# One encoder layer on one core: scaling the second group's rows in another stage, squares in a tile of their own, refills at other steps

## The chip, the core and the metric

The kernel runs on one core of a Trainium2 chip. The core has a matmul engine (TensorE, PE in the profile), VectorE (DVE), ScalarE (ACT), GpSimd (POOL) and SyncE (SP), which here issues nearly all DMA transfers. The engines run side by side. Each works through its own list of instructions in order, and an instruction that waits for a semaphore holds back all that stand behind it on that engine. SBUF is the memory on the chip, PSUM the accumulators that matmuls write, DRAM the memory outside.

The metric is the device time of one execution in microseconds (us), as the median of several runs. Before the change three runs took 1821.98, 1823.78 and 1827.82 us.

## The reference

One layer of a bidirectional encoder is applied to 1024 tokens (sample) and 256 tokens (prompt), model width 2048, all in float32:

```python
hn = rms_norm(x, norm_g)
proj = hn @ w_in                       # 2048 -> 4896 columns
xbc, z_ssd, dt_raw, q, k, v, z_att, mq, z_mem = split_cols(proj, IN_SIZES)
xbc = silu(centred_dwconv(xbc, conv_w, conv_b))       # 5 taps along the tokens
...                                    # SSD scans both ways, windowed attention,
...                                    # attention over 256 memory rows, gates
return x + concatenate([o_ssd, o_att, o_mem], -1) @ w_out
```

What matters here is the first line. `rms_norm(x, g)` divides each token's row by the root of its mean square plus 1e-6 and multiplies each feature by g. So the sum of squares of each token must be known before the token's features can be scaled for the product with `w_in`. The memory rows have such a norm too.

## The kernel before

**Products in two pieces.** Every operand of a large product is split into a high part (the value rounded to the matmul's reduced float32 form) and a low part (the remainder). A product is three matmuls: high x high, high x low, low x high. For the weights this is `wsplit` (lines 201 to 205): ACT writes the high part `wh`, DVE subtracts and writes the low part `wl`.

**Groups.** The 1280 tokens are worked in two groups of 640. `x_turned` holds x with features first, so a row tile is 128 features x 640 tokens, and there are 16 row tiles per group. `cur["H", q]` and `cur["L", q]`, q = 0 to 3, hold the two parts of four row tiles each.

**Token blocks.** `block_tok` (line 231) makes a product with 512 (or 288) weight columns for 4 or 5 token tiles: for each of 16 steps k it loads a weight tile `wraw` (three buffers), splits it (four buffers `wh` and `wl`), and issues three matmuls for each token tile. The last two steps are taken together.

**Stages of seven products.** `block_pair` (line 1182) makes two 128-column outputs over 640 tokens with a Strassen-like scheme: seven products instead of eight over halves of the features, tokens and columns. It has eight steps k per unit; each step is 21 matmuls of 320 columns. POOL makes three sums of weight tiles for it (`weight_sums`, line 1177, sums in `ws`), and ACT and DVE split them as `sh` and `sl` (three buffers). The sums of the rows, in the same scheme, are made by `p_sums` (line 1270) and split into `tH`, `tL` by `p_split` (lines 1276 and 1277). One stage has ten units (`units`, four gates and six convolution outputs), and there is one stage for each group. The evacuation of a unit (`ev_seven`) puts its first product into a tile `yu` of the pool `fin`, tag `xst`, with one buffer. The taps and gates of a unit are put into a list `left` and are issued a few at a time beside the next units.

**Order of the stages that the change touches.** Two memory blocks (`w_mem`); the q block of the first group, during which the rows of the first group are scaled and split (`p_step`); the first stage of seven products; the kv block and the mq block of the first group (token blocks), during which the rows of the second group are scaled, stored, summed and split (`t_step`), and in the end the first stage's rows in `cur` are replaced by those of the second group; the second stage of seven products. Then follow attention, SSD and the output products, which the change leaves alone.

**What feeds the second group's rows.** `stage_stats` reads the tokens of the second group (five tiles) and the memory rows (four tiles) in 36 pieces of 128 x 512, and ACT squares each with a running sum (line 1392). The piece lies in the same one buffer as `yu`. It is advanced at five of the seven points of each unit. When it is through, `x_rows(1)` spreads the reciprocal roots over a tile `rbc` (128 x 640). In the kv and mq blocks `p_load` then loads two row tiles of x, `p_scale` multiplies them by the gain and by `rbc` on DVE (line 1237) and stores them in DRAM (`xs_d`), `p_sums` and `p_split` follow. Later `r_load` reads the scaled rows back from `xs_d` and `r_fill` splits them into `cur` (lines 1248 and 1249), into new tiles. `t_plan` says at which step each of these is called.

**What sets the order.** The program is written step by step, but a scheduler of the tile framework sets the final order on each engine from the program's order, raised priorities (`tc.high_priority`) and its own idea of what is ready; `tc.issue_after(marks)` keeps an instruction behind the last weight split. A tile with one buffer makes the next writer wait for all readers of the last content.

Of the kernel before, what the change touches and what calls it, by code (L numbers as in the profile page):

```python
# [19 lines left out]
P = 128  # L20
# [21 lines left out]
def hymba_encoder_kernel(  # L42
# [223 lines left out]
    def block_feat(name, evac):  # L266

        ps = [[acc.tile([P, 512], F32, tag="acc", name="acc") for _ in range(2)] for _ in range(2)]
        src = laid_in(name)
        hls = {}  # L270
        for kk in range(KT // 2):
            raw = wp.tile([P, 512], F32, tag="wraw", name="wraw", bufs=RB)
            S.dma_start(raw, src[kk])
            with tc.high_priority(offset=HP[2]):
                h = wp.tile([P, 2, 256], F32R, tag="wh", name="wh", bufs=WB)
                l = wp.tile([P, 2, 256], F32R, tag="wl", name="wl", bufs=WB)
                wsplit(raw, h.rearrange("p a c -> p (a c)"), l.rearrange("p a c -> p (a c)"))
            hls[kk] = h, l
            if kk == KT // 2 - 2:
                continue  # L280
            tail = kk == KT // 2 - 1

            for kks in ([(kk - 1, kk)] if tail else [(kk,)]):
                for f in range(2):
                    for k in [2 * x + j for x in kks for j in range(2)]:
                        q, m = divmod(k, 4)
                        sh, sl = [x[:, k % 2, f * P:(f + 1) * P] for x in hls[k // 2]]
                        for half in range(2):
                            c = slice(half * 320, half * 320 + 320)
                            o = ps[f][half][:, :320]  # L290
                            T.matmul(o, sh, cur["H", q][:, m, c], start=(k == 0), stop=False)
                            T.matmul(o, sh, cur["L", q][:, m, c], start=False, stop=False)
                            T.matmul(o, sl, cur["H", q][:, m, c], start=False, stop=(k == KT - 1))
                    if tail and f == 0:
                        with tc.high_priority(offset=HP[1]):
                            evac(0, ps[0])
            for k in range(2 * kks[0], 2 * kk + 2):
                yield k
        with tc.high_priority(offset=HP[1]):
            evac(1, ps[1])  # L300


    def ev_gate(c, base):
# [5 lines left out]
        return f  # L309

    def ev_gateT(c, grp, f0):
        def f(fc, ps):
            z = ev.tile([P, 640], F32, tag="evu", name="zs")
            for b in range(2):
                zb, p = z[:, b * 320:b * 320 + 320], ps[b][:, :320]
                A.activation(zb, p, AF.Tanh, scale=0.5)
                V.scalar_tensor_tensor(out=zb, in0=zb, scalar=1.0, in1=p, op0=ALU.add, op1=ALU.mult)
            S.dma_start(zT_d[c][grp][:, f0 + fc, :], z)
        return f
# [24 lines left out]
    def conv_work(grp, fc, u):  # L344
# [5 lines left out]
        def first_tap():  # L350
            c.append(ev.tile([P, 650], F32, tag="evt", name="c")[:, :n])
            A.activation(c[0], u[:, :n], AF.Identity, scale=cw[0], bias=vec[:, R_CB + fc:R_CB + fc + 1])
# [26 lines left out]

    def ev_conv(grp, f0):  # L380
        us = []

        def f(fc, ps):
            fc = f0 + fc
            u = ev.tile([P, 650], F32, tag="evu", name="u")
            V.tensor_copy(u[:, 0:4], carry[:, fc, :])
# [6 lines left out]
            if len(us) == 2:  # L393
                left.extend(conv_two(*[conv_work(grp, f0 + i, us[i]) for i in range(2)]))
# [1369 lines left out]
```

## Time and profile before

| what | value |
|---|---|
| median of 3 runs | 1823.78 us (1821.98 to 1827.82) |
| the profiled execution | 1824.83 us |
| its span, first to last instruction | 1823.1 us |
| PE busy | 1778.3 us, 98% |
| DVE, ACT, POOL busy | 73%, 52%, 37% |
| granted PE clock, mean | 0.995 |
| DMA moved | 328.96 MB, 180 GB/s |

The profile is one execution. The page gives the busy time of each engine, a picture in 40 slices, the DMA queues, the chain of work that ended last, and the costliest groups of instructions. A group reads: line, engine, operation, output <- inputs, shape, number | busy us, mean ns of one | idle time of the engine just before them, and what ended it. A wait reads: who <- what ended it: us in total, times, longest. A row of the table of stretches reads: stretch in us, its length, then for each engine the busy us and the number of instructions, then the granted PE clock, the DMA share and GB/s. Matmuls are pipelined, so "busy" is not yet peak; the number of matmuls in a stretch shows better how fast they go.

### The profile page before, as it was taken

The numbers are of one execution on the slowest core, as the hardware profiler recorded it, in microseconds if no ns is written. First come the engines' busy times: TensorE is split into PE (matmuls) and PEld (weight loads), VectorE is DVE, ScalarE is ACT, GpSimd is POOL, SyncE is SP. The second block draws the span as 40 slices with busy tenths as digits, with TensorE's granted clock in tenths as the row PEclk, the third lists the DMA queues.
The fourth block names the chain that finished last, engine by engine and source line by source line (L and its number), as shares of the span: only waits on it lengthen the run. The fifth ranks groups of instructions, "written<-read, shape, count | busy, mean of one in ns | idle before, by whom it ended". The sixth has DMA issues, their size and how long they took to land.

```text
span 1823.1 us, 30989 instructions
## 1 busy us (share of the span) xinstructions
PE 1778.3 (98%) x10306; PEld 1572.7 (86%) x10306; DVE 1328.4 (73%) x2473; ACT 950.1 (52%) x2081; POOL 673.6 (37%) x1092
## 2 busy tenths in 40 slices
PE   9999999999999999999999999999999999999999
PEld 7788999999799999987777877887777787889998
DVE  5595678888878889787667767767787765766665
ACT  6554545553454444366567447666547644543332
POOL 0115778870168889411001110001111101048774
PEclk9999999999999999999999999999999999999999
DMA  8685544446853343374545577656688765654442
GB/s 296 196 315 192 152 142 146 128 146 206 265 189 91 114 117 110 106 219 133 162 136 155 165 241 267 207 173 213 220 282 259 238 212 161 201 154 147 142 139 81
DMA packets 213873, 328.96 MB, mean 180 GB/s; under 512 B 21904, under 2 KB 84688, under 8 KB 213712
## 3 DMA queue, kind: packets, MB, share of 16 engines
q1 hardware_dynamic: 213568, 326.92, 57.8%
q8 instruction: 81, 1.33, 0.3%
q14 instruction: 80, 0.66, 0.1%
q10 hardware_dynamic: 144, 0.06, 0.0%
HBM read 250.29 MB, written 76.61 MB: 179 GB/s over the span
## 4 chain that ended last, share of the span: by engine, by line
PE 65%; DMA 12%; issue 8%; DVE 6%; POOL 5%; ACT 3%; SPq 1%; ACTq 0%; POOLq 0%; DVEq 0%
PE acc L257 8%; PE acc L256 8%; PE acc L258 8%; PE acc L1207 7%; PE acc L1205 7%; PE acc L1206 7%; POOL ws L1177 3%; PE accm L1206 3%; PE accm L1205 3%; PE accm L1207 3%; PE py L937 2%; DVE wl L204 1%; DMA wraw<-in_w_in_pairs_dram 1%; DMA rf<-ac 1%; POOL wraw L1177 1%
## 5 line engine op out<-in xcount | busy, mean ns | idle before, releaser
L257 PE MATMUL acc<-wl,xH 128*128 128x512 f32 (+1 forms) x1248 | 479.0, 384 | 8.0 <-DVE wl L204 7.7
L256 PE MATMUL acc<-wh,xH 128*128 128x512 f32 (+1 forms) x1248 | 484.3, 388 | 1.6 <-ACT wh L203 1.5
L258 PE MATMUL acc<-wh,xL 128*128 128x512 f32 (+1 forms) x1248 | 476.0, 382 | 0.0
L204 DVE TENSOR_TENSOR wl<-wraw,wh 128x512 fp32r<-128x512 f32 (+1 forms) x480 | 351.8, 736 | 145.7 <-ACT wh L203 140.5
L203 ACT ACTIVATE wh<-wraw 128x512 fp32r<-128x512 f32 (+1 forms) x480 | 290.8, 612 | 211.1 <-PE acc L258 126.7
L257 PEld LDWEIGHTS acc<-wl,xH 128*128 128x128 f32 x1248 | 236.1, 189 | 54.9 <-DVE wl L204 13.6
L256 PEld LDWEIGHTS acc<-wh,xH 128*128 128x128 f32 x1248 | 236.1, 189 | 45.7 <-ACT wh L203 3.6
L258 PEld LDWEIGHTS acc<-wh,xL 128*128 128x128 f32 x1248 | 235.7, 189 | 42.1 <-issue 0.7
L1177 POOL TENSOR_TENSOR ws<-wraw 128x128 f32<-128x128 f32 x224 | 144.8, 646 | 340.9 <-DMA wraw<-in_w_in_pairs_dram 210.2
L203 ACT ACTIVATE sh<-ws 128x384 fp32r<-128x384 f32 x224 | 115.7, 523 | 272.9 <-PE acc L1206 131.2
L204 DVE TENSOR_TENSOR sl<-ws,sh 128x384 fp32r<-128x384 f32 x224 | 156.2, 700 | 136.9 <-ACT sh L203 132.5
L1177 POOL TENSOR_TENSOR ws<-wraw,ws 128x128 f32<-128x128 f32 x224 | 149.1, 666 | 17.3
L1177 POOL TENSOR_TENSOR ws<-ws,wraw 128x128 f32<-128x128 f32 x224 | 152.8, 682 | 0.0
L1177 POOL TENSOR_TENSOR wraw<-wraw 128x128 f32<-128x128 f32 x224 | 138.9, 620 | 17.5
L645 POOL COPY lg<-nsink 128x2 f32<-128x2 f32 x40 | 17.3, 433 | 268.9 <-PE ppt L673 138.9
L1205 PE MATMUL acc<-xH,wh 128*128 128x320 f32 x320 | 99.5, 311 | 3.7 <-ACT wh L203 3.7
L1207 PE MATMUL acc<-xH,wl 128*128 128x320 f32 x320 | 99.2, 310 | 3.3 <-DVE wl L204 3.3
L1205 PE MATMUL acc<-tH,sh 128*128 128x320 f32 x320 | 99.1, 310 | 1.0 <-ACT qs L324 1.0
L1207 PE MATMUL acc<-tH,sl 128*128 128x320 f32 x320 | 99.2, 310 | 0.0
L1206 PE MATMUL accm<-tL,wh 128*128 128x320 f32 x320 | 99.1, 310 | 0.0
L1205 PE MATMUL accm<-tH,wh 128*128 128x320 f32 x320 | 99.0, 310 | 0.0
L1206 PE MATMUL acc<-xL,wh 128*128 128x320 f32 x320 | 99.0, 309 | 0.0
(479 smaller groups left out, 3921.1 us busy)
## 6 DMA issues: line engine op xcount, KB each, us to landing
wraw<-in_w_in_pairs_dram SPq DMA_DIRECT2D x160, 256.0 KB, 2.8
wraw<-in_w_in_laid_dram SPq DMA_DIRECT2D x128, 256.0 KB, 3.7
wraw<-in_w_out_laid_dram SPq DMA_DIRECT2D x64, 256.0 KB, 3.3
wraw<-in_w_out_pairs_dram SPq DMA_DIRECT2D x64, 256.0 KB, 2.9
xH<-xH SPq DMA_DIRECT2D x16, 640.0 KB, 5.9
xL<-xL SPq DMA_DIRECT2D x16, 640.0 KB, 6.5
rf<-ac SPq DMA_DIRECT2D x40, 256.0 KB, 4.0
rb<-ac SPq DMA_DIRECT2D x40, 256.0 KB, 4.4
```

The costliest lines, as they stand in the source:

```text
L203: a = A.activation(h, raw, AF.Copy)
L204: b = V.tensor_sub(l, raw, h.bitcast(F32))
L256: T.matmul(ps[t][:, :n], sh, h[:, :n], start=(k_ == 0), stop=False)
L257: T.matmul(ps[t][:, :n], sh, l[:, :n], start=False, stop=False)
L258: T.matmul(ps[t][:, :n], sl, h[:, :n], start=False, stop=(k_ == last))
L645: G.tensor_copy(lg[:, :, nk:nk + 1], ns8[:, rr, :].unsqueeze(2))
L937: T.matmul(py[:, h * 64:h * 64 + 64], mt[:, (h % 4) * P:(h % 4 + 1) * P], xsT[g][:, h * 64:h * 64 + 64], start=True, stop=True)
L1177: G.tensor_tensor(out=o, in0=x, in1=y, op=op)
L1205: T.matmul(ps[p], h, xh, start=(k_ == 0), stop=False)
L1206: T.matmul(ps[p], h, xl, start=False, stop=False)
L1207: T.matmul(ps[p], l, xh, start=False, stop=(k_ == 7))
```

## The change

- The squares get a tile of their own (tag `sq`, one buffer) and are made in two lots: the five token tiles of x beside the first stage of seven products (`first_side`), the four memory tiles beside the second (`next_side`). They are advanced one piece at a time with no grouping. In the first stage the side work is advanced at five points of a unit in the first four units and at seven in the other six; in the second stage at three.
- After its squares, `first_side` runs `x_rows(1)` and then, for each of the 16 row tiles, loads it from `x_turned` into the tile `sq`, scales it on DVE, and stores it in `xs_d`.
- In the kv and mq blocks the second group's rows are loaded from `xs_d` instead of `x_turned` (`p_next`), and neither scaled nor stored there. In the plan the loads of the first four pairs stay where they are and those of the other four come one step earlier; the sums of the first four stay, the others come one step earlier; the splits of the first four come one step later, the others stay; the refills stand at steps 25, 26, 27, 28, 29, 31, 33 and 35 instead of 25, 27, 29, 31, 32, 33, 35 and 37, and they write into the tiles that are there.
- Within one step the calls are sorted: split, refill, sums, loads.
- Three functions that nothing calls are taken out (`block_feat`, `ev_gateT`, `ev_conv`); small tiles move from the pool `sm` to `mp`, and some tiles of 650 columns become 646 or 640.

```diff
-    def p_load(k, grp=0):
+    def p_load(k, src):
         raw[k] = [rp.tile([P, 640], F32, tag="ch", name=n, bufs=CH) for n in ("ra", "rb_")]
         for i in range(2):
-            r = k + 8 * i
-            S.dma_start(raw[k][i], x_turned[grp, r * P:(r + 1) * P, :])
-
-    def p_scale(k, grp=0):
-
-        for i, x in enumerate(raw[k]):
-            r = k + 8 * i
-            V.scalar_tensor_tensor(out=x, in0=x, scalar=vec[:, R_G + r:R_G + r + 1], in1=rbc, op0=ALU.mult, op1=ALU.mult)
-            if grp:
-                S.dma_start(xs_d[r], x)
-
-    def p_rows(k, tiles):
+            S.dma_start(raw[k][i], src(k + 8 * i))
+
+    def x_row(grp, r):
+        return x_turned[grp, r * P:(r + 1) * P, :]
+
+    def scale_row(r, x):
+        V.scalar_tensor_tensor(out=x, in0=x, scalar=vec[:, R_G + r:R_G + r + 1], in1=rbc, op0=ALU.mult, op1=ALU.mult)
+
+    def p_rows(k, tiles, new=True):
         for i, x in enumerate(tiles):
             q, j = divmod(k + 8 * i, 4)
-            if j == 0:
+            if new and j == 0:
                 new_quad(q)
...
     def r_fill(k):
-        p_rows(k, again.pop(k))
+        p_rows(k, again.pop(k), new=False)
...
+    def p_first(k):
+        p_load(k, lambda r: x_row(0, r))
+
+    def p_next(k):
+        p_load(k, lambda r: xs_d[r])
...
     t_plan = {}
     for k in range(8):
-        at = (3, 6, 9, 12, 15, 17, 19, 21)[k]
-        for j, f in ((at - 2, lambda k: p_load(k, 1)), (at, lambda k: p_scale(k, 1)), (at + 1, p_sums), (at + 2, p_split)):
+        at = (4, 7, 10, 13, 15, 17, 19, 21)[k]
+        for j, f in ((at - 3, p_next), (at, p_sums), (at + 2, p_split)):
             t_plan.setdefault(j, []).append((f, k))
-    for k, at in enumerate((25, 27, 29, 31, 32, 33, 35, 37)):
+    for k, at in enumerate((25, 26, 27, 28, 29, 31, 33, 35)):
         for j, f in ((at - 2, r_load), (at, r_fill)):
             t_plan.setdefault(j, []).append((f, k))
...
-    def stage_stats():
-        yield from stats([(xrow(t), t) for t in range(5, 10)] + [(mrow(i), 10 + i) for i in range(4)],
-                         lambda i: fin.tile([P, 512], F32, tag="xst", name="sst"), ahead=1, group=3)
+    def square_place(_):
+        return fin.tile([P, 640], F32, tag="sq", name="sst")[:, :512]
+
+    def first_side():
+        yield from stats([(xrow(t), t) for t in range(5, 10)], square_place, ahead=1)
+        for _ in x_rows(1):
+            yield
+        for r in range(KT):
+            x = fin.tile([P, 640], F32, tag="sq", name="xrow")
+            S.dma_start(x, x_row(1, r))
+            yield
+            with ExitStack() as st:
+                for ins in marks:
+                    st.enter_context(tc.issue_after(ins))
+                scale_row(r, x)
+                S.dma_start(xs_d[r], x)
+            yield
+
+    def next_side():
+        yield from stats([(mrow(i), 10 + i) for i in range(4)], square_place, ahead=1)
...
-    def pairs_in(grp, extra):
+    def pairs_in(grp, extra, side):
...
-                if k in (0, 2, 4, 5, 7):
-                    next(squares, None)
+                if grp == 0 and (u > 3 or k not in (3, 7)) or grp and k in (0, 2, 4):
+                    next(side, None)
...
-    pairs_in(0, p_step)
-    for _ in squares:
-        pass
-    for _ in x_rows(1):
-        pass
+    side = first_side()
+    pairs_in(0, p_step, side)
```

More of the change, by code (lines that the diff above doesn't have):

```diff
@@ L264, in block_tok @@
             yield k
[L266 to L300, printed above, removed]
     def ev_gate(c, base):
@@ L308, in f @@
             S.dma_start(z_d[c][base + i], z)
[L309 to L318, printed above, removed]
         return f
@@ L1251, in p_fill @@
     def p_fill(k):
-        p_scale(k)
+        for i, x in enumerate(raw[k]):
+            scale_row(k + 8 * i, x)
         p_rows(k, raw[k])
@@ L1312, in t_step @@
                 weight_sums(w_in_pairs, (j - 27) // 2)
-            for f, k in t_plan.get(j, ())[::-1]:
+            for f, k in sorted(t_plan.get(j, ()), key=lambda x: ((p_split, r_fill, p_sums, p_next, r_load).index(x[0]), x[1])):
                 f(k)
@@ L1330, in begin @@
             else:
-                tiles = [ev.tile([P, 650], F32, tag="evu", name="r") for _ in range(2)]
+                tiles = [ev.tile([P, 640], F32, tag="evu", name="r") for _ in range(2)]
             r0, r1 = [hv(x[:, o:o + 640], 2) for x in tiles]
@@ L1579, in hymba_encoder_kernel @@
         extra=left_and(lambda k: t_step(16 + k)))
-    pairs_in(1, t_step)
+    side = next_side()
+    pairs_in(1, t_step, side)
+    assert next(side, None) is None
     early.close()
```

47 lines of the change are left out of this document (16 added, 31 removed).

## The prediction

> **What bounds the kernel now.** I read the engine totals first, then a table of stretches cut at the stages, then who waited for whom in the stretches that the change touches, and last single instructions there.
>
> ```profile
> span 1823.1 us, 30989 instructions
> PE 1778.3 (98%) x10306; PEld 1572.7 (86%) x10306; DVE 1328.4 (73%) x2473; ACT 950.1 (52%) x2081; POOL 673.6 (37%) x1092
> ```
>
> TensorE (PE) is the bound; whatever is gained must come out of the 45 us in which it does not work. The next table (stretch in us from the start of the span; busy us and number of instructions of each engine; granted clock; DMA share; GB/s) holds, in order, the second memory block, the q block, the first unit of the first stage of seven products, its units two to four, its units five to ten, the kv block, the mq block, and the second stage of seven products.
>
> ```profile
> 60.00:93.00 33.00, 32.53 (x146) 25.92 (x145) 22.19 (x38) 19.17 (x38) 2.77 (x6) 1.00 0.68 211
> 93.00:147.00 54.00, 53.18 (x234) 43.42 (x232) 46.77 (x77) 27.20 (x44) 9.34 (x12) 1.00 0.87 307
> 147.00:172.00 25.00, 22.70 (x138) 21.11 (x138) 10.85 (x19) 12.58 (x25) 13.64 (x23) 1.00 0.64 211
> 172.00:250.00 78.00, 76.90 (x521) 75.96 (x520) 53.72 (x86) 38.48 (x79) 58.35 (x98) 1.00 0.50 145
> 250.00:405.00 155.00, 149.03 (x995) 146.68 (x994) 126.32 (x190) 80.72 (x165) 130.46 (x201) 0.99 0.47 137
> 405.00:442.00 37.00, 37.00 (x278) 37.00 (x277) 28.63 (x51) 13.16 (x26) 3.96 (x7) 1.00 0.53 162
> 442.00:510.00 68.00, 62.19 (x265) 49.05 (x264) 55.15 (x85) 29.93 (x50) 13.43 (x20) 0.95 0.84 276
> 510.00:757.00 247.00, 247.00 (x1687) 246.63 (x1686) 206.01 (x330) 115.93 (x205) 199.78 (x296) 1.00 0.39 115
> ```
>
> The second stage of seven products loses nothing: 1687 matmuls in 247 us, 0.1464 us each, so 21 of them, one step k of a unit, are 3.07 us. At that pace the 521 matmuls of units two to four need 76.3 of their 78 us (lost: 1.7) and the 995 of units five to ten 145.7 of 155 (lost: 9.3). The mq block idles 5.8 us and runs at a granted clock of 0.95, another 3.4 us of 68: 9.2. The other stretches idle 0.5, 0.8, 2.3 and 0. Together 23.8 us lie in reach of this change, 1.3%.
>
> What PE waits for there is the weight split on ScalarE (ACT, line 203) and VectorE (DVE, line 204):
>
> ```profile
> PE acc L257 <- DVE wl L204: 6.5, 10, 1.4
> PE acc L1205 <- ACT wh L203: 3.7, 5, 1.2
> PE acc L1207 <- DVE wl L204: 3.3, 7, 0.8
> ```
>
> In the first stage the split is late behind the squares of stage_stats. The first row is their group between 145 and 440 us; then three squares with their waits, and the matmul that stood after them:
>
> ```profile
> L1392 ACT ACTIVATE sst<-sst 128x512 f32<-128x512 f32 x36 | 22.7, 631 | 53.7 <-DMA sst<-in_mem_sample_dram 14.8 <-DMA sst<-in_x_sample_dram 13.8 <-DMA sst<-in_mem_prompt_dram 12.3
> ...
> 190.91 0.63 ACT L1392 ACTIVATE sst<-sst 128x512 f32<-128x512 f32 x1 [3.65 <-DMA sst<-in_x_sample_dram]
> ...
> 194.72 0.63 ACT L1392 ACTIVATE sst<-sst 128x512 f32<-128x512 f32 x1 [2.15 <-DMA sst<-in_x_sample_dram]
> ...
> 198.49 0.63 ACT L1392 ACTIVATE sst<-sst 128x512 f32<-128x512 f32 x1 [2.11 <-DMA sst<-in_x_sample_dram]
> ...
> 200.20 0.41 PE L1205 MATMUL acc<-xH,wh 128*128 128x320 f32 x1 [0.76 <-ACT wh L203]
> ```
>
> Each square waits for a load that is issued only when the square before has freed the one buffer: 3.8 us from square to square, where PE consumes a step in 3.07. Three or four in a row eat ACT's lead (three buffers of sh, so at most three steps, 9.2 us), and PE stops. SyncE (SP) is held too, because the buffer is also that of the evacuation (yu):
>
> ```profile
> SPq L1401 <- ACT sst L1392: 35.4, 23, 3.2
> SPq L1401 <- DVE u L1351: 22.1, 5, 5.8
> SPq L1401 <- DVE r L1351: 16.0, 4, 5.0
> ```
>
> In the mq block (440 to 505 us) ACT stands behind DVE, and behind POOL's sums for the next stage:
>
> ```profile
> ACT tH L1276 <- DVE ra L1270: 14.9, 7, 3.8
> ACT sh L203 <- POOL ws L1177: 6.6, 2, 4.0
> ```
>
> **The change part by part.** Prices come from these rows: the weight split and a tap in the first stage, the same split and a scaling in the mq block, then transfers (first stage, its later part, mq block; KB, us from issue to landing).
>
> ```profile
> L204 DVE TENSOR_TENSOR wl<-wraw,wh 128x512 fp32r<-128x512 f32 x82 | 67.1, 823 | 10.1 <-ACT wh L203 9.9
> L357 DVE SCALAR_TENSOR_TENSOR c<-u,vec,c 128x638 f32<-128x638 f32 x46 | 44.5, 970 | 0.1
> ...
> L204 DVE TENSOR_TENSOR wl<-wraw,wh 128x512 fp32r<-128x512 f32 x16 | 11.2, 699 | 0.0
> L1237 DVE SCALAR_TENSOR_TENSOR ra<-ra,vec,rbc 128x640 f32<-128x640 f32 x6 | 5.4, 898 | 0.6 <-DMA ra<-in_x_turned_dram 0.6
> ...
> sst<-in_x_sample_dram SPq DMA_DIRECT2D x12, 256.0 KB, 3.3
> ra<-in_x_turned_dram SPq DMA_DIRECT2D x2, 320.0 KB, 3.0
> ...
> xbc_d<-u SPq DMA_DIRECT2D x6, 319.0 KB, 3.6
> zT<-th SPq DMA_DIRECT2D x4, 320.0 KB, 2.8
> ...
> xs<-ra SPq DMA_DIRECT2D x6, 320.0 KB, 3.7
> ```
>
> *Squares of x move forward.* With a place of their own they wait for nothing of the first stage, and in the order of the built program the 20 squares stand earlier: seven in the second memory block, eight in the q block, five in the first unit, none in units two to four. Units two to four then equal the second stage, which loses nothing: -1.7. In the memory block three squares follow each other one weight row apart, 12 matmuls at 33/146 us, 2.7 us, where load and square take 3.3+0.63+0.15=4.1 (3.8 in the rows above): 3 x 1.4=4.2 us, less ACT's lead; between 0 and 4, and I take +1.5, since the squares of x_stats end just before and leave little lead. In the q block DMA is 0.87 busy; eight more 256 KB loads are 2 MB in 54 us, 39 GB/s on 307. Loads get slower, weights too: 0 to 5, I take 2. In the first unit four intervals are short by 4.1-3.07: 4 us less lead; 0 to 4, I take 1.
>
> *Scaling moves to units five to ten.* Sixteen loads, scalings (line 1237 today) and stores go through one buffer, as one chain: scaling 0.98 (the tap's 0.97; 0.90 in the mq block, where POOL rests), store 2.8, load 3.0, three hand-overs of an estimated 0.1: 7.1 us; 7.9 with the 3.6 of xbc_d. From the first to the last scaling stand 34 steps in the order, 104.4 us of PE, 7.0 us for each of 15 gaps. DVE had 126.3 us of work for 145.7 us of matmuls, so 91 us here; 15 scalings make 105.7: DVE is full. In order it also waits where a gap holds less work than the chain is long. By the durations of such rows (split 0.82, tap 0.97 and their like) the gaps hold 5.0, 8.9, 7.0, 4.8, 6.6, 9.3, 8.1, 5.5, 8.4, 9.0, 4.0, 10.7, 8.2, 5.8, 5.2 us; a chain of 7.1 leaves waits of 2.1+0.1+2.3+0.5+1.6+3.1+1.3+1.9=12.9. So DVE is 12.9+1.3=14 us too long, its wl is queued behind each wait, and three steps of lead take 9.2: PE loses 5, against 9.3 today, -4.3. The bounds are 0 (stores land faster) and 20 (7.9 in the chain, no lead). SP waits about 3 us for each store to land before it issues the next load, and weight loads stand behind; it stood 73.5 us behind line 1401 in today's rows, and 16 x 3=48 take their place. I leave that within the bounds. There are 16 transfers more than before, because the rows are read twice from DRAM afterwards.
>
> The Trainium skill, "DMA: Bandwidth & Descriptors" (Anatomy of one DMA), gives about 2.0 us fixed plus bytes over 436e3; its fit is for the GpSimd path. An estimate from it is 2.75 us for 320 KB, a chain of 6.8 and a sum about 2 us lower; the rows, 2.8 to 3.6, are longer. The Trainium skill, "SBUF — State Buffer" (Who interferes with whom), says that a VectorE instruction with two SBUF inputs contends with a GpSimd one that reads SBUF: it speaks against putting the scaling beside POOL's sums. The trace agrees, 823 ns for wl there and 699 ns where POOL rests; by the smaller price the sum would be 1.4 us lower.
>
> *Squares of mem.* They are called in the second stage, but stand earlier in the built order: five in the tenth unit, nine in the kv block, two in mq. From the first to the fourteenth there are 13 intervals, 53 us at 4.1, while PE needs 4 steps of 3.07 and 15 of 2.0 (15 matmuls at 37/278 us): 42.3. ACT's lead covers 9.2 of the 10.7: PE loses 1.5, between 0 and 11 with no lead. I take 2, where nothing is lost today.
>
> *kv and mq blocks.* Sixteen scalings and 16 stores leave. Twelve of them stood in the mq stretch, 12 x 0.90=10.8 of DVE's 55 us, and ACT's 14.9 us behind line 1270 shrink. Refills start in place and reach k=7 two steps earlier. What is late next is the sums for the next stage: the third set of weights is still loaded behind refills and its sh stands before the split of mq's row 14. I take 3 us for 9.2, between 0 and 9.2: -6.2.
>
> *Nothing:* the functions taken out are not called; small tiles change pool; tiles of 650 become 640 or 646.
>
> Sum: +1.5+2+1-1.7-4.3+2-6.2=-5.7. The profiled execution took 1824.83 us (span and 1.7 around it), 1.05 above the median of 1823.78: 1819.1, and 1818 for the median.
>
> **The rivals.** *The row chain binds.* Chain 7.9, no lead: units five to ten lose 20 in place of 5, the sum is +9.3, 1833. For it: DVE is full by the rows. Against: the second stage runs with 206 of 247 us of DVE and no loss. It decides against the change as soon as that part loses 10.7. Chance 0.17. *The squares bind.* One mechanism, ACT paced at 4.1 us a square without lead, in four places: +4, +5, +4, +11, with -1.7-4.3-6.2 it is +12, 1836. For it: the three squares at 190 to 198 us. Chance 0.11. *The end of mq is not mended*, since ACT still waits for POOL there: +0.5, 1824. Chance 0.10. *All is covered:* first stage, kv and mq lose what the second stage does, almost nothing: -14 to -20, 1807. Chance 0.17.
>
> **How the numbers follow.** The forecast has 0.45, with 0.28 beyond 0.3% (5.5 us, about what this measurement can tell from no change) and 0.17 within. Faster: 0.28+0.17=0.45; same: 0.17+0.10=0.27; slower: 0.17+0.11=0.28. The range of 8 in 10 goes from 1807, all covered, to 1833, the row chain; the forecast's own is 1812 to 1823.
>
> **What would show it.** Squares on ACT before 172 us and from about 380 on, none between; no PE wait in units two to four; DVE waiting for xrow loads of 1 to 3 us in about half of the scalings; PE waiting for wl in units five to ten by some 5 us; ACT waiting for sst in the kv block; the clock at 1.00 in the mq block. I am wrong if DVE's waits for rows exceed 20 us, if PE stops in the kv block for more than 5 us, or if mq still ends with a half-clock stretch.

## The result and the profile after

The changed kernel takes 1841.84 us in the median of four runs (1837.20 to 1843.13), the kernel before 1823.50: a ratio of 1.0092, 95% interval 1.0067 to 1.0117. (The ratios in this document are estimated from all runs of both kernels; the quotient of the two medians, here 1.0101, can differ.) The forecast was 1818, its range 1807 to 1833. The change makes the kernel 17 us slower by the ratio.

The top of the page after, and its table of stretches, cut where the same matmuls stand at which a stage or a unit begins (columns as in the table of before): memory block, q block, unit one, units two to four, units five to ten, kv, mq, second stage of seven products.

```profile
span 1841.4 us, 31026 instructions
PE 1787.4 (97%) x10306; PEld 1577.7 (86%) x10306; DVE 1327.5 (72%) x2473; ACT 951.4 (52%) x2081; POOL 676.7 (37%) x1092
```

```profile
60.00:102.00 42.00, 39.10 (x166) 29.78 (x167) 24.54 (x42) 25.34 (x57) 4.61 (x8) 1.00 0.71 224
102.00:166.00 64.00, 58.52 (x241) 46.30 (x240) 46.58 (x78) 31.99 (x61) 12.76 (x24) 0.95 0.84 291
166.00:191.00 25.00, 25.00 (x171) 24.77 (x171) 13.82 (x26) 14.76 (x32) 16.09 (x29) 1.00 0.72 238
191.00:265.00 74.00, 74.00 (x508) 74.00 (x507) 56.97 (x86) 33.84 (x61) 63.16 (x98) 1.00 0.36 113
265.00:427.00 162.00, 154.07 (x1019) 150.23 (x1018) 138.57 (x202) 68.97 (x129) 125.91 (x177) 0.99 0.54 170
427.00:470.00 43.00, 36.44 (x239) 34.57 (x238) 28.26 (x55) 20.87 (x49) 3.88 (x8) 0.92 0.67 200
470.00:526.00 56.00, 55.52 (x246) 45.50 (x245) 41.15 (x71) 29.95 (x52) 13.95 (x22) 1.00 0.79 259
526.00:773.00 247.00, 246.20 (x1681) 245.75 (x1680) 199.69 (x320) 112.97 (x199) 196.60 (x296) 1.00 0.36 108
```

PE now idles 2.9 us in the memory block, 5.5 in the q block, 7.9 in units five to ten and 6.6 in the kv block, whose clock falls to 0.92. Units one to four and the mq block idle next to nothing: these two are better than before.

PE issues nearly the same matmuls in the same order in every kernel here, so a second reading needs no bounds at all: take the start of the same matmul in two traces and see by how much it comes later. The distance grows where time is lost. The table gives, in us, how much each stretch is longer (+) or shorter (-) than in the profile of before, one execution of each kernel. The kernels below the second row are those of the experiments.

| kernel | to the first stage | units 1 to 4 | 5 to 8 | unit 9 | unit 10, kv | mq | second stage | rest |
|---|---|---|---|---|---|---|---|---|
| changed | +12.0 | -7.3 | +1.7 | +6.8 | +9.3 | -8.7 | +1.8 | +2.8 |
| changed, again | +10.7 | -7.3 | +1.5 | +6.5 | +9.6 | -8.3 | +1.6 | +1.6 |
| x_held | +4.4 | -7.2 | +6.1 | +6.4 | +6.5 | -6.4 | +1.2 | +6.0 |
| mem_held | +13.3 | -7.3 | +2.3 | +6.7 | -3.2 | -6.4 | +1.5 | +2.3 |
| both_held | -3.6 | -5.9 | +5.6 | +6.7 | -3.8 | -7.1 | +2.1 | +2.7 |
| squares_own | +10.4 | +2.9 | -3.6 | +0.1 | -1.6 | -0.9 | +1.6 | +8.5 |
| no_load | -0.5 | -3.7 | +2.5 | +6.4 | +7.2 | -7.1 | +1.5 | +2.1 |
| plan_only | +0.4 | -1.7 | -1.3 | +0.2 | +0.4 | -1.5 | +2.0 | +0.9 |
| old_rows | +3.9 | -7.0 | -1.0 | 0.0 | +0.3 | -2.6 | +3.4 | +3.1 |
| no_scaling | +4.6 | -7.3 | +0.7 | +0.6 | -2.6 | -7.6 | +1.1 | +4.4 |
| prx_apart | +4.9 | -7.3 | +1.4 | +6.8 | -3.8 | -6.0 | +1.2 | +3.1 |
| half_rows | +8.3 | -7.3 | +0.6 | +0.4 | -1.8 | +2.4 | +0.5 | +2.2 |
| half_rows_prx | +3.6 | -7.0 | -3.3 | +2.1 | -2.8 | +0.4 | +0.5 | +2.5 |
| rows_apart | -2.3 | -6.0 | +0.9 | +1.8 | -0.5 | -5.8 | +1.6 | +3.6 |
| tiles_moved | +2.9 | -3.9 | +0.2 | 0.0 | -1.0 | -1.2 | +1.1 | +5.5 |

How far one execution may be trusted is in the table too. tiles_moved has the instructions of before in the order of before (but for two short neighbours on DVE), and still differs by 2.9, 3.9 and 5.5 us in three stretches; the eight kernels whose squares of x are held (x_held, both_held, old_rows, no_scaling, prx_apart, half_rows, half_rows_prx, rows_apart) lie between -3.6 and +8.3 in the first column. Most of that spread arises in the last three steps of the q block: six of the eight lose 3.4 to 6.0 us there and tiles_moved 3.5, and the granted clock halves there in each of these traces, while it doesn't in both_held, rows_apart and the kernel before. Up to the start of these three steps the eight lie between -2.0 and +2.4, and the four kernels whose squares of x run ahead with their loads (changed, changed again, mem_held, squares_own) between +6.2 and +7.6. The execution that was profiled can also be an outlier: that of x_held took 1841.87 us, 7 above its median. Among kernels that share the part in question, unit nine repeats within 0.4 us (6.4 to 6.8), unit ten with kv and mq within about 3. The last column is above zero for all, tiles_moved included, so the 2.8 us of the changed kernel there aren't put down to the change.

Where does the time go? Three losses and two gains: the way to the first stage (+12), unit nine (+7), unit ten and kv (+9); units one to four (-7) and mq (-9). ACT's squares in the first and third of these, the groups of instructions by line (count, busy us, mean ns, idle time before and what ended it), from 60 to 192 us and from 400 to 492 us of the changed kernel:

```profile
L1332 ACT ACTIVATE sst<-sst 128x512 f32<-128x512 f32 x20 | 12.6, 628 | 28.0 <-DMA sst<-in_x_sample_dram 15.6 <-DMA sst<-in_x_prompt_dram 12.3
...
L1332 ACT ACTIVATE sst<-sst 128x512 f32<-128x512 f32 x16 | 10.1, 629 | 25.6 <-DMA sst<-in_mem_sample_dram 15.9 <-DMA sst<-in_mem_prompt_dram 9.8
```

ACT waits 28.0 and 25.6 us in front of squares, for their loads, more than twice what the squares take. What that does is seen in the list of single instructions in the kv block, first ACT, then PE:

```profile
426.46 0.63 ACT L1332 ACTIVATE sst<-sst 128x512 f32<-128x512 f32 x1 [2.57 <-DMA sst<-in_mem_sample_dram]
427.00 0.18 ACT L1332 ACTIVATION_READ_ACCUMULATOR sst<-sst 128x1 f32 x1
430.65 0.63 ACT L1332 ACTIVATE sst<-sst 128x512 f32<-128x512 f32 x1 [3.46 <-DMA sst<-in_mem_sample_dram]
431.18 0.19 ACT L1332 ACTIVATION_READ_ACCUMULATOR sst<-sst 128x1 f32 x1
431.27 1.09 ACT L203 ACTIVATE wh<-wraw 128x288 fp32r<-128x288 f32 x3
...
431.75 0.40 PE L256 MATMUL acc<-wh,xH 128*128 128x288 f32 x1 [2.86 <-ACT wh L203]
```

Between 427.2 and 430.65 ACT does nothing but wait; three weight tiles are ready behind the square (it splits all three at once at 431.27), and PE stands 2.9 us for the first.

### The profile page after: what moved, and what is told of

Its sections match the earlier page's. It is cut to its first block, busy times and chain, and to the rows that moved or that the text cites. A ratio compares the mean times of both kernels' runs of the same rounds, so it can differ in the third digit from the quotient of the medians.

```text
span 1841.4 us, 31026 instructions
## 1 busy us (share of the span) xinstructions
PE 1787.4 (97%) x10306; PEld 1577.7 (86%) x10306; DVE 1327.5 (72%) x2473; ACT 951.4 (52%) x2081; POOL 676.7 (37%) x1092
## 4 chain that ended last, share of the span: by engine, by line
PE 67%; DMA 13%; DVE 8%; issue 4%; ACT 3%; POOL 3%; SPq 1%; ACTq 0%; DVEq 0%; POOLq 0%
PE acc L257 8%; PE acc L258 8%; PE acc L256 8%; PE acc L1143 8%; PE acc L1141 8%; PE acc L1142 8%; PE accm L1141 3%; PE accm L1142 3%; PE accm L1143 3%; DVE wl L204 2%; PE py L873 2%; DMA sst<-in_x_sample_dram 1%; POOL ws L1113 1%; DMA wraw<-in_w_in_pairs_dram 1%; DMA rf<-ac 1%
## 5 line engine op out<-in xcount | busy, mean ns | idle before, releaser
L1113 POOL TENSOR_TENSOR ws<-wraw,ws 128x128 f32<-128x128 f32 x224 | 154.9, 691 | 17.5
L1113 POOL TENSOR_TENSOR ws<-ws,wraw 128x128 f32<-128x128 f32 x224 | 148.7, 664 | 0.0
L1142 PE MATMUL acc<-tL,sh 128*128 128x320 f32 x320 | 98.7, 308 | 0.0
```

The costliest lines, as they stand in the source:

```text
L1113: G.tensor_tensor(out=o, in0=x, in1=y, op=op)
L1142: T.matmul(ps[p], h, xl, start=False, stop=False)
```

## The experiments

Each ratio is to the kernel before on the same chip, whose median there was 1822.9 us (1 to 3 and plan_only), 1827.3 (4 and the rest of 6), 1826.8 (5, 7, half_rows and half_rows_prx) and 1825.7 (rows_apart and the changed kernel again); 0.001 is 1.8 us.

**1 to 3. The squares held where the program calls them.** The built order had let them run ahead of their calls: of x into the memory and q blocks, of mem into unit ten, kv and mq. Each square is tied behind the latest weight split; the arithmetic is the same.

```diff
-                    A.activation(x, x, AF.Square, accum_out=s4[:, c:c + 1])
+                    with ExitStack() as st:
+                        for ins in marks if held else ():
+                            st.enter_context(tc.issue_after(ins))
+                        A.activation(x, x, AF.Square, accum_out=s4[:, c:c + 1])
```

x_held sets `held` in `first_side`, mem_held in `next_side`, both_held in both. In the traces two of the held squares of x still stand in the q block, and one of mem late in mq.

> The changed kernel, with the 20 squares of x kept behind the weight split beside which the program calls them, so that they run in the first stage of seven products and not in the memory and q blocks. Matched by the same matmuls, the changed kernel is 7.4 us behind at the end of the q block and 12.0 us behind at the first matmul of the first stage. Theory: those 12 us are the early squares (one buffer, ACT and SP held at each); they go, and 0 to 4 us come back in units one to four, where a square every 3.8 to 4.1 us stands beside steps of 3.07: 1830 to 1834 us. Rival (the weights and rows for the first stage come late for another reason, not the squares): still 10 to 12 us behind at the first matmul of the first stage, 1840 to 1843 us.

> The changed kernel, with the 16 squares of the memory rows kept behind the weight split beside which the program calls them, so that they run in the second stage of seven products and not in unit ten, the kv and the mq block. From unit ten to the start of mq the changed kernel falls behind from 12.1 to 22.5 us. Theory: these 10 us are the squares of mem in the kv block, which go, and the second stage, with DVE and ACT well below full, takes them for 0 to 3: 1831 to 1834 us. Rival (the kv block is late behind the taps and gates that unit ten left, and the loads of rows): kv still loses 8 us or more, 1839 to 1843 us.

> The changed kernel with both lots of squares held behind the weight split where the program calls them. Theory (squares are the loss, the row chain costs what the trace shows, some 6 us at unit nine): 12 and 10 us go, 0 to 6 come back: 1819 to 1826 us, level with the kernel before. Rival (row chain and DVE are the loss): 1836 us or more, with PE waiting for wl in units five to ten for more than 10 us.

Measured: x_held 1834.72, ratio 1.0067 (1.0045 to 1.0089); mem_held 1833.18, 1.0041 (1.0024 to 1.0058); both_held 1823.93, 1.0011 (0.9998 to 1.0023). The squares of mem cost 9 to 10 us: 1.0092 to 1.0041, and 1.0067 to 1.0011; unit ten and kv go from +9.3 to -3.2. In the second stage 14 of them stand in the stretch 526 to 773 us of mem_held, without any idle time in front:

```profile
L1335 ACT ACTIVATE sst<-sst 128x512 f32<-128x512 f32 x14 | 8.6, 615 | 0.0
```

The squares of x cost less than expected: 1.0092 to 1.0067, and 1.0041 to 1.0011, about 5 us with intervals that reach from near 0 to 10. In the profile of x_held 8 us go in front, but 4 come back in units five to eight, where experiment 7 finds a wait of PE. With both held the kernel is level with the one before: what the change loses in all goes with the place of its squares. The rival, row chain and DVE as the main loss, doesn't hold, though unit nine's 6.7 us stay.

**4. One part of the change alone, the squares' own tile.** The kernel before, with:

```diff
-                         lambda i: fin.tile([P, 512], F32, tag="xst", name="sst"), ahead=1, group=3)
+                         lambda i: fin.tile([P, 512], F32, tag="sq", name="sst"), ahead=1, group=3)
```

and the small tiles in the other pool, to make room.

> The kernel before, with one part of the change: the 36 squares in a tile of their own (called at the points of before, not held; small tiles in the other pool to make room). In the built order 8 squares come into the second memory block, 7 into the q block, 3 into the first unit, 18 into units two to four, none after. Theory (a square that comes once per weight step or oftener paces ACT at about 4 us; one per two steps costs nothing): 8 to 13 us lost by the first unit as in the changed kernel, 0 to 6 more in units two to four, where 16 squares of mem stand beside 24 steps, and units five to ten gain what the squares cost there, 3 to 7: 1828 to 1836 us. Rival (the early squares hurt only together with the other parts): 1816 to 1824 us.

Measured: 1836.99, ratio 1.0056 (1.0032 to 1.0079), 10 us slower. The way to the first stage is 10.4 us longer, as in the changed kernel, without any of its other parts but the small tiles. In units one to four, with the 16 squares of mem, +2.9 stands against -7.3 in the kernels that have them elsewhere.

**5. ACT's time or the load.** The changed kernel, with the 20 squares of x reading a tile that is in SBUF; their loads are left out, and so the second group's norm is not that of x.

```diff
-                    A.activation(x, x, AF.Square, accum_out=s4[:, c:c + 1])
+                    A.activation(x, x if loaded_ else rbc[:, :512], AF.Square, accum_out=s4[:, c:c + 1])
```

> The changed kernel, whose 20 squares of x read the tile rbc, which stands in SBUF, instead of a loaded piece; their loads are left out (so the second group's norm is wrong). In the built order the 20 squares stand even closer, beside ten weight steps of the second memory and the q block. Theory (a square costs PE time through the wait for its load in the one buffer, with ACT and SP held): at most 3 us behind the kernel before at the first matmul of the first stage, where the changed kernel is 12.0 behind, and 1828 to 1833 us beside a kernel before at 1823. Rival (ACT's 0.8 us for each square is what is too much): 8 us or more behind there, 1837 to 1842 us.

Measured: 1833.95, ratio 1.0035 (1.0018 to 1.0051), 10 us less than the changed kernel's ratio. The first stage begins 0.5 us ahead of before. The squares take as long as ever, but ACT waits 1.6 us in front of all 20 of them; the stretch is 60 to 160 us:

```profile
L1332 ACT ACTIVATE sst<-rbc 128x512 f32<-128x512 f32 x20 | 12.5, 625 | 1.6 <-DVE rbc L1409 1.4
```

So it is the wait for the load that costs, not the 0.8 us of work. The experiment takes away ACT's wait, SP's wait for the buffer and 5 MB of traffic at once; which of the three counts most isn't told apart.

**6. The plan, the scalings, and the tiles.** plan_only is the kernel before with the refills in place and at the new steps (first part of the code below). tiles_moved is the kernel before with the small tiles and the tile sizes of the changed one. old_rows is both_held with the rows loaded, scaled and stored in kv and mq, by the steps of before. no_scaling is both_held without `scale_row` in `first_side`: rows are loaded and stored, but the second group's norm is left out (second part).

```diff
-    for k, at in enumerate((25, 27, 29, 31, 32, 33, 35, 37)):
+    for k, at in enumerate((25, 26, 27, 28, 29, 31, 33, 35)):
...
-                scale_row(r, x)
                 S.dma_start(xs_d[r], x)
```

> The kernel before, with only two parts of the change: the refills into the tiles that are there and at steps 25, 26, 27, 28, 29, 31, 33, 35. Scaling, storing and squares stay as before. The changed kernel gains 7.5 us against the one before across the mq block. If the gain comes from the refills' place, this kernel gets 5 to 7 us: 1816 to 1819. If it comes from the scalings and stores that left the mq block, it gets 0 to 2 us: 1821 to 1824, and ACT still waits for DVE's sums in the mq block for some 15 us.

> The kernel before, with nothing but the small tiles in the other pool and the tiles of 650 columns cut to 646 and 640. The order of instructions on every engine is that of before. Predicted at nothing: 1821 to 1825 us. Rival (the addresses in SBUF matter, since the changed kernel loses 2.8 us from the end of the second stage to the end of the span with the same order there): 2 to 4 us slower, 1825 to 1828.

> The kernel with both lots of squares held, and the second group's rows loaded, scaled and stored in the kv and mq blocks as before, with the steps of before; what is left of the change is squares in a tile of their own, held where the program calls them, and refills into the tiles that are there. With both lots held, the kernel is 9.5 us ahead of before at unit five, loses 10.2 from there to kv and gains 8.8 from kv to the second stage. Theory (the scalings beside the first stage cost more there than they save in mq): from unit five to kv it now loses 0 to 5, in kv and mq it gains 0 to 2 in place of 8.8: 1813 to 1819 us, ahead of both. Rival (moving the scalings is worth it, only the squares hurt): the mq block's gain goes, and nothing comes back before: 1828 to 1832 us.

> The kernel with both lots of squares held, without the 16 multiplications beside the first stage: the rows are loaded into the one buffer and stored in DRAM unscaled (so the second group's norm is left out of its products). The chain of load and store stays, DVE has 16 us less. With the multiplications the stretch from the start of unit eight to kv falls behind the kernel before by 4.1 us, nearly all of it in unit nine, where PE waits 2.7 us for wl and the clock halves. Theory (DVE is full and its wl late): this loss goes, -1 to +1 us there. Rival (SP, held by the chain of load and store, delivers the weights late): 3 us or more stay, with ACT or POOL waiting for wraw.

Measured: plan_only 1.0005 (0.9991 to 1.0019), tiles_moved 0.9998 (0.9981 to 1.0014), old_rows 0.9995 (0.9979 to 1.0011), no_scaling 0.9945 (0.9927 to 0.9964).

The plan alone gains 1.5 us in mq, the kernels in which the scalings left it gain 6 to 9. The waits of ACT in the mq block, by what ended them, plan_only (442 to 512 us) and then the changed kernel (470 to 526 us), say the same:

```profile
ACT tH L1276 <- DVE ra L1270: 14.3, 7, 4.2
ACT sh L203 <- POOL ws L1177: 6.7, 2, 4.2
```

```profile
ACT tH L1210 <- DVE ra L1204: 7.1, 3, 3.5
ACT sh L203 <- POOL ws L1113: 6.2, 2, 3.5
```

The wait for DVE's sums halves with the scalings gone; the wait for POOL is as long as before. The small tiles cost nothing that can be measured. For old_rows I had expected 1813 to 1819, and this missed: units five to nine are 13.3 us better than in both_held (-1.0 against +12.3), but unit ten with kv is 4.1 worse, mq 4.5, and the way to the first stage came out 7.5 worse in this execution. The ratios of old_rows and both_held can't be told apart: by the times, scaling the rows beside the first stage costs there about what it saves in kv and mq. no_scaling shows the price of the 16 multiplications: 0.9945 against 1.0011, 12 us, for 16 us of DVE's time. What PE waits for between 336 and 400 us in both_held:

```profile
PE acc L1143 <- DVE wl L204: 3.3, 3, 2.7
PE acc L1141 <- DVE r L1289: 0.3, 1, 0.3
```

and without the multiplications, with load, store and buffer as they were:

```profile
PE accm L1141 <- DVE r L1291: 0.3, 1, 0.3
```

Unit nine goes from +6.7 to +0.6. The chain of loads and stores through the one buffer alone isn't what costs there; a full DVE is. Between the same matmuls, unit nine holds 27.7 us of DVE's work in both_held (359.3 to 390.5 us) and 22.3 in no_scaling (361.1 to 386.2), where PE at its own pace of 3.07 us a step needs 24.6. Unit seven, with four scalings as well, holds 24.8 and is 27.4 us long.

**7. A matmul that waits for a PSUM buffer.** Once the squares are held, units five to eight lose 6 us. There PE waits in front of a matmul that spreads the reciprocal roots. The list of both_held, PE and then DVE:

```profile
264.68 0.30 PE L1142 MATMUL acc<-tL,sh 128*128 128x320 f32 x1
268.26 0.35 PE L1410 MATMUL prx<-identr,rx 128*128 128x128 f32 x1 [3.28 <-POOL ws L1113]
...
266.63 0.88 DVE L204 TENSOR_TENSOR wl<-wraw,wh 128x512 fp32r<-128x512 f32 x1
267.44 0.68 DVE L1411 COPY rbc<-prx 128x512 f32<-128x512 f32 x1
```

The row names POOL, but POOL's last root was done at 250.9 us. The matmul starts 0.14 us after DVE's copy of the first four spread blocks ends, and two of the three buffers of that pool hold a unit's `accm`: it waits for the buffer that the copy frees, and the copy stood behind DVE's other work. prx_apart puts two steps between the copy and the last matmul (`last_mm` is the latest matmul of the unit), and with it every scaling two points later:

```diff
+                    if grp and o:
+                        st.enter_context(tc.issue_after(last_mm[0].ins))
                     T.matmul(ps[:, i * P:(i + 1) * P], rx[:, t:t + 1].broadcast_to([P, P]), ident, start=True, stop=True)
             V.tensor_copy(rbc[:, o * P:(o + n) * P], ps[:, :n * P])
+            if grp and o == 0:
+                yield
+                yield
```

> The kernel with both lots of squares held, in which the last of the five matmuls that spread the reciprocal roots stands behind the matmuls of a later step. There PE waited 3.3 us for it, and the clock halved for 7.8 us; by the order the matmul waits for the PSUM buffer that DVE's copy of the first four frees, and that copy stood in DVE's queue. Theory: the wait goes and the halved clock with it, 3.3 + 3.9 = 7 us less in units five to seven: 1815 to 1819 us beside a kernel before at 1823. Rival (POOL, which the row of waits names, is what was late): the wait only moves, 1821 to 1825.

Measured: 1823.55, ratio 0.9985 (0.9973 to 0.9997), 5 us less than both_held by the ratios (7 expected). The 7 counted a clock halved for 7.8 us; the trace of both_held has one such spell there, of 3.41 us, worth 1.7, and 3.3 + 1.7 is 5.0. Units five to eight go from +5.6 to +1.4, and the view of waits lists none of PE between 262 and 300 us. POOL as the cause falls.

**8. How many scalings, and where.** half_rows is both_held with only eight rows scaled beside the first stage, one every four points; the others are loaded, scaled and stored in mq. half_rows_prx adds the edit of prx_apart. rows_apart is prx_apart, with all 16 rows, but the side work rests at four points of unit nine. The first part of the code is half_rows, the second rows_apart:

```diff
-        for r in range(KT):
+        for r in (0, 8, 1, 9, 2, 10, 3, 11):
...
-                if grp == 0 and (u > 3 or k not in (3, 7)) or grp and k in (0, 2, 4):
+                if grp == 0 and (u > 3 or k not in (3, 7)) and (u != 8 or k not in (2, 3, 4, 5)) or grp and k in (0, 2, 4):
```

> The kernel with both lots of squares held, with the rows of only four of the eight pairs scaled beside the first stage, one every four points of a unit; the other eight rows are loaded, scaled and stored in the mq block. Theory (DVE is full beside the first stage once a scaling stands in every second step): unit nine's 6.7 us go, 2 to 5 come back in mq: 1818 to 1823 us. Rival (scalings cost the same in either place): 1823 to 1826.

> Both of these edits together. By the theories 4 and 7 us less than with both lots of squares held: 1811 to 1816 us, faster than both kernels; by the rivals 1821 to 1826.

> The kernel with both lots of squares held and the last spreading matmul apart, in which the side work isn't advanced at four points of unit nine: two of the four scalings that stood beside its steps, and those behind them, come later, the last beside the end of unit ten. With four scalings in unit nine every kernel fell 6.4 to 6.9 us behind from the start of unit nine to the start of unit ten, and without scalings 0.6. Theory (unit nine, with the taps of two convolutions and two gates, has no DVE time for four scalings; the ninth and tenth together have): 0 to 2 us behind in unit nine, 0 to 3 more in unit ten: 4 to 6 us less than with the matmul apart alone, a ratio of 0.995 to 0.997 to the kernel before. Rival (sixteen scalings are too much anywhere in units eight to ten): the loss moves to unit ten, 5 to 7 us, ratio 0.998 to 0.999.

> The changed kernel once more, for its stretches in a second profiled execution. Theory (the losses are in its order, not in one execution): 8 us or more behind the kernel before at the first matmul of the first stage, 6 to 7 us in unit nine, 8 to 10 us from unit ten to the start of mq, 6 to 9 us ahead in mq; a ratio of 1.007 to 1.012. Rival (they are spells of one execution): some of these missing.

Measured: half_rows 0.9995 (0.9977 to 1.0013), half_rows_prx 0.9987 (0.9972 to 1.0002), rows_apart 1821.84, 0.9978 (0.9965 to 0.9992), the changed kernel again 1841.34, 1.0086 (1.0069 to 1.0103). Half the rows: unit nine's loss is gone (+0.4), and mq gives more than its gain back (+2.4 in place of -7.1, where 2 to 5 us were expected); whether that is worth anything the times don't tell. Both edits together missed: 0.993 to 0.996 was expected, and 0.9987 is what the rival said. rows_apart missed narrowly (0.995 to 0.997 expected). With two of the four scalings moved out of unit nine, that unit loses 1.8 instead of 6.8 and mq keeps its 5.8, but unit ten with kv goes from -3.8 to -0.5: of the 5.0 us saved in unit nine 3.3 are lost behind it, so the rival, that the loss moves on, holds in part. The ratios of rows_apart and prx_apart, 0.9978 and 0.9985, can't be told apart; that four scalings were too many for that one unit is seen in the profile alone. rows_apart is 4 us faster than the kernel before (1.5 to 6.4 by the interval) and, on the same chip, 1821.84/1841.34 = 0.989 of the changed one. Units five to ten and kv of rows_apart, with the granted clock at 1.00 where the changed kernel had 0.99 and 0.92:

```profile
251.00:408.00 157.00, 152.56 (x1021) 148.95 (x1020) 141.00 (x202) 65.39 (x118) 130.58 (x180) 1.00 0.54 165
408.00:442.00 34.00, 33.21 (x246) 32.23 (x244) 26.21 (x51) 14.46 (x29) 1.80 (x4) 1.00 0.59 182
```

The second profile of the changed kernel has every loss and gain of the first in its place, within 1.3 us.

## Why the prediction was wrong

By the table the changed kernel's profile is 18.4 us behind, where 5.7 ahead were forecast: 24.1 apart. The two terms for squares make up 14 of these (+10.4 and +10.1 for +4.5 and +2), the term for scaling in units five to ten 12 (+7.7 for -4.3), and 4.6 came in the stages behind, for which I had nothing; units two to four and mq came out 6.5 better than forecast.

**Squares of x move forward** (+4.5 to unit one's end) failed in its discount. The pace was right in the memory block, 4.1 us from square to square in the median, and slower in the q block, about 6. But I took off "ACT's lead", at most three steps and 9.2 us, and so chose +1.5 out of 0 to 4 in the memory block and +1 out of 0 to 4 in unit one; for the q block I chose +2 out of 0 to 5. Measured: +4.4 in the memory block, more than the upper end; +7.4 in the q block, of which 4.6 come in its last three steps, where six of the eight kernels with these squares held lose about as much; and -1.6 in unit one. The squares of x thus cost some 7 us in front, twice what I took. The lead can be read in the trace: the time from the end of a weight's high part on ACT to the first matmul that uses it, for each of the 16 steps of a block.

| lead, us | before: mean (least, most) | changed: mean (least, most) | both_held: mean (least, most) |
|---|---|---|---|
| second memory block | 2.9 (0.1, 5.8) | 1.4 (0.1, 3.8) | 3.1 (0.1, 5.8) |
| q block | 3.7 (0.9, 5.9) | 2.4 (0.1, 5.9) | 4.5 (2.1, 5.9) |
| kv block | 3.2 (1.3, 6.7) | 1.5 (0.1, 5.3) | 2.9 (1.4, 5.7) |

Before, with no square of the second group there, the lead was 2.9 to 3.7 us in the mean, and in the memory block 0.1 to 0.9 us for five steps on end. Buffers bound a lead; they don't say that it is there.

**Squares of mem** (+2, bound 11) failed at the same place. In kv a step takes 2.0 us, so the same buffers hold less time, and the lead that was there was 3.2 us, not 9.2. Measured for unit ten and kv 9.3 and 9.6, against -3.2 and -3.8 with the squares held; kv alone is 10.1 longer than before.

These two were the rival "the squares bind", with +4+5+4 and +11. It had a chance of 0.11 because the lead was taken to cover most of them; its 1836 was also too low, since the term for scaling failed as well.

**Scaling moves to units five to ten** (-4.3) failed in size and in sign. The chain was better than predicted: stores landed in 2.2 us, not 2.8, and DVE waited 8.1 us for rows, not 12.9. PE waited 4.9 us for wl, where 5 were expected, which is luck: DVE's waits, from which the 5 were worked out, came out a third shorter. And 2.9 of the 4.9 came in one piece in unit nine, where the clock halved. The matmuls that spread the reciprocal roots had moved into this stage too; they were in no term, and PE waited 1.5 us for them here (3.3 in both_held). Waits of PE in units five to ten, and PE around the long one:

```profile
PE acc L1143 <- DVE wl L204: 4.9, 5, 2.9
PE prx L1407 <- POOL ws L1113: 1.5, 1, 1.5
```

```profile
390.62 0.31 PE L1142 MATMUL acc<-xL,wh 128*128 128x320 f32 x1
393.80 0.41 PE L1143 MATMUL acc<-xH,wl 128*128 128x320 f32 x1 [2.88 <-DVE wl L204]
...
389.03 0.76 DVE L204 TENSOR_TENSOR wl<-wraw,wh 128x512 fp32r<-128x512 f32 x1 [0.65 <-ACT wh L203]
390.75 0.06 DVE L1269 MEMSET u<- 128x2 f32 x1 [0.95 <-DMA xbc_d<-u]
390.81 0.67 DVE L204 TENSOR_TENSOR sl<-ws,sh 128x384 fp32r<-128x384 f32 x1
391.85 1.04 DVE L1172 SCALAR_TENSOR_TENSOR xrow<-xrow,vec,rbc 128x640 f32<-128x640 f32 x1 [0.36 <-DMA xrow<-in_x_turned_dram]
392.81 0.93 DVE L204 TENSOR_TENSOR wl<-wraw,wh 128x512 fp32r<-128x512 f32 x1
```

The wl that PE needs stands behind a memset that waits 0.95 us for a store of taps to land, and behind a scaling of 1.04 us. I had spread DVE's excess over 34 steps; most of it fell on one unit, the ninth, which has 27.3 us of DVE's work with its taps, gates and four scalings and is 31.4 us long (369.5 to 400.9). Leaving the 16 scalings out of both_held is worth 12 us. The bound on the other side, 20 us, held.

**Units two to four** (-1.7) were right in kind: no wait of PE, and no square from 189 to 405 us. The size was off because my stretches were cut at round numbers, unit two at 172 and unit five at 250. By the matmuls these units began at 180.4 and 259.9 in the trace of before, 79.5 us for 24 steps of 3.07, and lost 5.7; so part of what I had booked for units five to ten (9.3, in fact 6.9 to kv) lay here. The same round numbers took the last 7 us of the q block, which ends at 154.0, for unit one.

**kv and mq blocks** (-6.2, between -9.2 and 0) was right: -8.7 and -8.3 in mq, and the clock in mq is 1.00. That POOL's sums for the next stage would be late next was right too: ACT waits 6.2 us for them, as before. The gain comes from the scalings that left, as argued, and hardly from the refills' steps; but it isn't 0.90 us for each, since half_rows, with eight of them in mq, has no gain there at all.

**Nothing** for pools and tile sizes held, 0.9998 (0.9981 to 1.0014).

Of the conditions under which I said I would be wrong, one came true: PE stops more than 5 us in kv (6.6 of 43 idle).

What stays open: which part of the early squares' cost is ACT's wait and which is SP's, which holds weight loads behind the next square's load; and what decides whether the end of the q block falls into a half-clock spell, which happens with and without early squares.

## What to carry to other kernels

A side task that waits for its own load on an engine which feeds PE can cost PE nearly all by which its interval exceeds PE's steps (unit ten and kv lost 9.3 us where the bound without any lead was 11), so put a price on it without any lead, unless the trace shows the lead at that place. Giving a task its own buffer also frees the scheduler to run it early: look where the built order puts it, and hold it where it was meant to be. An engine's excess over a stage isn't spread evenly; look for the one unit in which everything falls together, since a long stop of PE can bring a half-clock spell behind it, as the next section shows.

## What was not expected of the hardware

A stop of PE has a second price. Windows of the changed kernel, in two pairs, right after the stops at 390.62 (2.88 us) and 428.60 (2.86 us); the number after the engines is the granted clock:

```profile
394.80:398.00 3.20, 3.20 (x13) 3.20 (x13) 2.44 (x4) 0.00 (x0) 1.79 (x3) 0.50 0.82 189
398.20:402.20 4.00, 4.00 (x30) 4.00 (x29) 3.16 (x6) 1.73 (x3) 3.52 (x6) 1.00 0.55 211
432.40:435.60 3.20, 3.20 (x14) 3.20 (x15) 3.07 (x6) 0.46 (x1) 0.00 (x0) 0.50 0.88 247
435.80:440.00 4.20, 4.20 (x34) 4.20 (x33) 1.48 (x4) 1.82 (x5) 2.54 (x6) 1.00 0.35 105
```

PE is busy all the time, with 13 matmuls in 3.2 us where the next window has 30 in 4.0. By this trace's record of the clock each such spell lasts 3.41 or 6.83 us, so by an estimate from that record it costs another 1.7 or 3.4 us, half its length; a stop of 2.9 us is then worth 4.6. In the changed kernel's trace every one of the seven spells ahead of the last microseconds begins in or within 2 us after a stop of 1.4 to 3.6 us, while ten stops of 1.0 to 1.6 us had none behind them, so the length of a stop alone doesn't decide it. The Trainium skill, "TensorE: Matmul & The Clock Gate" (Part 1), speaks of a free-running window of 3413 ns and of half rate after an idle window of that length: the length of the spells agrees, but stops of 2.9 us, and some of less than 2, were enough here.
